# A hybrid decoder layer on one core: the first three column blocks in eight equal pieces, and the sample attention's cache tiles three to a visit

## The chip, the core and the metric

The kernel runs on one core of one Trainium2 chip. The time is device microseconds of one launch, median of 3 runs: 1757.73 us, between 1757.28 and 1758.61. One more execution, under the profiler, took 1758.0 us, and its span from the first to the last instruction is 1756.2 us.

In the profile PE is the tensor engine (matmuls), PEld its weight loads, DVE the vector engine, ACT the scalar engine, POOL the GpSimd engine, SP the engine that issues most loads and stores; a small q behind a name is that engine's own queue of DMA issues.

## The reference

One layer for a prompt group (256 tokens) and a sample group (8 sequences of 4 tokens), 288 tokens in all, in float32.

```python
z = jnp.einsum('ntd,de->nte', x, w_in)
h, gate_b, gate_c, q, k, v, g_a, g_b = jnp.split(z, _split_points(), axis=-1)

ya, conv_mix_new = _causal_dwconv(gate_c * h, conv_mix_prev, w_conv_mix)
ya = gate_b * ya
...
for g, (win, dil) in enumerate(GROUPS):
    ...
    o, l = _dilated_band_prompt(q[:, :, g], kg, vg, slopes[g], dil)   # prompt
    ...
    o, l = _dilated_band_sample(q[:, :, g], kg, vg, slopes[g], dil)   # sample: keys, values from a cache
wg = jax.nn.softmax(jnp.stack(lses), axis=0)
yb = jnp.einsum('gnth,gnthd->nthd', wg, jnp.stack(outs))

mixed = jax.nn.sigmoid(g_a) * (ya @ w_branch_a) + jax.nn.sigmoid(g_b) * (yb @ w_branch_b)
x1 = _layernorm(ALPHA * x + mixed @ w_out, ln1_g, ln1_b)
a, b = jnp.split(x1 @ w_up, 2, axis=-1)
a, conv_ffn_new = _causal_dwconv(a, conv_ffn_prev, w_conv_ffn)
y = _layernorm(ALPHA * x1 + (jax.nn.silu(a) * b) @ w_down, ln2_g, ln2_b)
```

The model width is 2048, the inner width of the last part 5632; there are 3 groups of 4 heads of 128. The old cache rows are also copied to the outputs.

## The kernel before, in words

**Layout.** Features lie on the 128 partitions, tokens along the free axis. Each token row is kept as two halves of 144 (dimensions h and a in the code: half and place in it). A matmul reads them interleaved ("p a h").

**Products.** Every weight matrix is cut into column blocks of 128. A block is 16 k-tiles of 128x128, 1 MB, loaded into a buffer `wst` (three of them, `prepare`, L169 on). Each float32 number is split in two parts: ACT rounds it to fp32r (`hi`), DVE subtracts that from the number (`lo`); `split`, L223, does it for weights and for activations. `product` (L197) then issues three matmuls for each k-tile: hi by hi, hi of the weights by lo of x, lo of the weights by hi of x (L217 to L219), 48 for a block, into one accumulator. Split weights go to half blocks `whi` and `wlo`, four buffers of each, so that the casts run up to two blocks ahead of PE. ACT's cast of a half block waits until PE has freed a buffer.

**The start.** PE first runs `N_WARM` matmuls on zeros (L235). The first three column blocks (0 and 1 together in `w_two`, 2 in `w_one`) are computed together as x arrives: `FIRST` cuts the 16 k-tiles into four pieces of two and two of four. For each piece there is a load of x (the first four on ACT's queue, the others on SP's), one of `w_two` and one of `w_one` (SP), then three casts on ACT in the order x, blocks 0 and 1, block 2, and three subtractions on DVE in that order. `first_three` (L285 is its matmul) goes piece by piece; in a piece it takes the three kinds of term one after the other, in each the k-tiles, and for each k-tile the three blocks. At its beginning it calls `prepare`, which issues the load of block 3 behind those loads on SP.

**What follows.** The q blocks (12, with the first three), then 24 blocks of k and v by head, each head followed by the prompt's attention in three parts spread over later products; then the gated convolution (48 blocks), the two branches with their gates, the output projection with a norm, and the up and down projections in three parts with the last norm.

**Sample attention.** It runs in between, as a generator (`sample_steps`) that `product` advances: 20 steps over the blocks from k on (`N_STEP`, `N_STEP_BLOCKS`), about one in five products. The old keys and values come as 18 tiles each of 128x2048 (`fetch_two`, L424: two at a time, each loaded into one of two `cache` buffers and then stored to the output from there, L425). For the scores, DVE masks q by batch (`by_batch`, one operation of 128x1024 for a group, L412), and PE multiplies with 32 columns of weights for each batch and head (L450), four heads beside each other in the array; the sums are picked and get their bias (`pick_t`, L431). After the last keys come the softmax, transposes (L483, L485, L493), and the same again with the values (L506), the last with the new values (L513). These matmuls are float32; each appears as two records in the trace. A group of matmuls that `in_a_row` ties together is called a visit here: PE leaves the stream of products for it. The first visit of a half reads two tiles with four batches each, the others two tiles with one batch each.

**SP's order.** All weight loads, cache loads and cache stores go through SP's queue in program order as scheduled; a store waits there for its load to land, a cache load for PE to be done with the buffer, a weight load for DVE to be done with it.

Of the kernel before, what the change touches and what calls it, by code (L numbers as in the profile page):

```python
# [11 lines left out]
F32R = mybir.dt.float32r  # L12
# [5 lines left out]
P = 128  # L18
# [11 lines left out]
HX = 160  # L30
# [23 lines left out]
C_M0 = C_TM + NT  # L54
C_M1 = C_M0 + NG * P
# [31 lines left out]
def layer_kernel(ctx: ExitStack, tc: tile.TileContext, ins, outs):  # L87
# [40 lines left out]
    spent = [0]  # L128
# [42 lines left out]
    def prepare():  # L171
# [24 lines left out]
    def product(x):  # L196

        w = w_ready.pop(0)
        if not w_ready:
            prepare()  # L200
        if steps_on[0]:
            spent[0] += N_STEP
            while spent[0] >= N_STEP_BLOCKS:
                spent[0] -= N_STEP_BLOCKS
                next(steps, None)
        o = acc(x[0].shape[-1])
        mms(o, w, x)
        prompt_step()
        return o.rearrange("p a h -> p h a")
# [27 lines left out]

    xh = sb(big, [P, KD, 2, HX], "xh", F32R)
    xl = sb(big, [P, KD, 2, HX], "xl", F32R)
# [6 lines left out]
    w_two_lo = [sb(wk, [P, 2, HK, P], "cache", F32R, bufs=2) for _ in range(2)]  # L246
# [4 lines left out]
    for k0, n, queue in FIRST:  # L251
        k = slice(k0, k0 + n)
        (act if queue == "act" else sp).dma_start(xs[:, k], x_in[:, k])
        sp.dma_start(w_two[:, :, k], w_in_two[:, :, k])
        sp.dma_start(w_one[:, k], w_in_one[:, k])
    splits = []
    for k0, n, _ in FIRST:
        k = slice(k0, k0 + n)
        splits.append(split(xh[:, k, :, :H], xl[:, k, :, :H], xs[:, k].rearrange("p k (a h) -> p k h a", h=2)))
        h = slice(k0 % HK, k0 % HK + n)  # L260
        splits.append(split(w_two_hi[:, :, k], w_two_lo[k0 // HK][:, :, h], w_two[:, :, k]))
        splits.append(split(w_one_hi[k0 // HK][:, h], w_one_lo[k0 // HK][:, h], w_one[:, k]))
    for before, after in zip(splits, splits[1:]):
        for i in range(2):
            behind(after[i], before[i])
# [3 lines left out]
    def first_three():  # L269
# [10 lines left out]
        for k0, n, _ in FIRST:  # L280
            for term in range(3):
                for k in range(k0, k0 + n):
                    xk = x[term == 1][:, k].rearrange("p h a -> p a h")
                    for b in range(3):
                        i = pe.matmul(  # L285
                            o[b], first_w(term == 2, b, k), xk, start=k == 0 and term == 0, stop=k == KD - 1 and term == 2
                        )
                        if before is not None:
                            behind(i, before)
                        before = i  # L290
        return [t.rearrange("p a h -> p h a") for t in o]

    cst = sb(big, [P, C_M0], "cst")
# [107 lines left out]
    bmask = cst[:, C_BM : C_BM + NB * NS].rearrange("p (b r) -> p b r", b=NB)  # L401
    tmask = cst[:, C_TM : C_TM + NT]

    sw = sb(wk, [P, NH * NB * NS + 1152], "sw", bufs=1)
    sw_m = sw[:, : NH * NB * NS].rearrange("p (j b r) -> p j b r", j=NH, b=NB)
    sw2 = sw[:, NH * NB * NS :]

    def by_batch(src):

        m = sw_m  # L410
        shape = [P, NH, NB, NS]
        dve.tensor_tensor(m, src.unsqueeze(2).broadcast_to(shape), bmask.unsqueeze(1).broadcast_to(shape), ALU.mult)  # L412
# [608 lines left out]
```

## Time and profile before

| | before |
|---|---|
| median of 3 runs | 1757.73 us (1757.28 to 1758.61) |
| profiled execution: time | 1758.0 us |
| profiled execution: span | 1756.2 us |
| PE busy | 1738.8 us, 99% |
| DVE busy | 1006.7 us, 57% |
| ACT busy | 797.9 us, 45% |
| POOL busy | 243.7 us, 14% |
| mean granted PE clock | 0.996 |
| read from and written to HBM | 389.89 MB and 94.53 MB |

How to read the lines below. A row of the timeline has the start, the duration, the engine and line, the operation, what it writes and reads, how many instructions were merged, and in brackets how long the engine stood idle before and what released it. A row of a group has the count, the shortest, median and longest duration in nanoseconds, and the first and the last start. Matmuls overlap in the array: a matmul of 288 columns has a duration of 286 ns while one starts every 0.12 us. A row of the chain of waits has a start, a time and what filled it; it shows the step from one matmul to the next. A row of waits has who waited for whom, the total in us, the number and the longest. A row of a stage (a window of the span) has the length, the busy time of PE, PEld, DVE, ACT and POOL with their instructions, the granted clock, the share of DMA time and GB/s.

### The profile page before, as it was taken

The page shows a single profiled execution, that of the slowest core. Times are in us where ns is not written, and L with a number is a line of the kernel's source. Part 1 is how long each engine was busy: PE and PEld are TensorE (multiplying, and loading weights), DVE is VectorE, ACT ScalarE, POOL GpSimd, SP SyncE. Part 2 cuts the span into 40 slices and gives each one's busy share as a digit, 9 for nine tenths or more (in the row PEclk, how much of TensorE's full clock was granted, in tenths as well). Part 3 has the DMA queues.
Part 4 walks back from the last instruction along what each step waited for, and adds up shares of the span by engine and source line. Part 5 has one row for each costly group of instructions (what it writes and reads, how often), then busy time and mean ns, then how long its engine had stood idle before and what let it go on. Part 6 is the DMA issues. An engine that isn't in the chain of part 4 may idle for free.

```text
span 1756.2 us, 33518 instructions
## 1 busy us (share of the span) xinstructions
PE 1738.8 (99%) x14257; PEld 1710.7 (97%) x14257; DVE 1006.7 (57%) x1278; ACT 797.9 (45%) x1142; POOL 243.7 (14%) x404
## 2 busy tenths in 40 slices
PE   9999999999999999999999999999999999999996
PEld 9999999999999999999999999999999999999996
DVE  5444445555555444455588888765555555555554
ACT  5444444334434333344455655544454443345444
POOL 0000000000000000001165333300011110011165
PEclk9999999999999999999999999999999999999998
DMA  9477787787787877477766656566666666666662
GB/s 330 170 287 274 274 307 283 280 326 282 299 322 272 319 300 264 150 252 264 259 251 224 231 219 231 224 226 230 224 232 221 235 218 238 219 236 217 225 217 102
DMA packets 61350, 436.25 MB, mean 248 GB/s; under 512 B 7312, under 2 KB 9360, under 8 KB 17296
## 3 DMA queue, kind: packets, MB, share of 16 engines
q1 hardware_dynamic: 59472, 429.40, 66.4%
q10 hardware_dynamic: 1728, 4.72, 0.7%
q8 instruction: 111, 1.82, 0.4%
q14 instruction: 39, 0.32, 0.1%
HBM read 389.89 MB, written 94.53 MB: 276 GB/s over the span
## 4 chain that ended last, share of the span: by engine, by line
PE 99%; DMA 0%; DVE 0%; ACT 0%; SPq 0%; ACTq 0%; issue 0%; DVEq 0%
PE acc L217 32%; PE acc L219 31%; PE acc L218 31%; PE long L506 1%; PE long L450 1%; PE acc L285 1%; DMA dd<-in_w_in 0%; PE att L391 0%; ACT yah L747 0%; DVE dd L723 0%; PE att L351 0%; PE acc L383 0%; PE att L349 0%; PE att L374 0%; PE att L687 0%; PE att L686 0%
## 5 line engine op out<-in xcount | busy, mean ns | idle before, releaser
L223 DVE TENSOR_TENSOR wlo<-wst,whi 128x1024 fp32r<-128x1024 f32 (+2 forms) x584 | 709.1, 1215 | 613.1 <-ACT whi L223 607.6
L223 ACT CAST whi<-wst 128x1024 fp32r<-128x1024 f32 (+2 forms) x584 | 593.3, 1017 | 888.0 <-PE acc L218 777.7
L217 PE MATMUL acc<-xh,whi 128*128 128x288 f32 (+1 forms) x3216 | 922.8, 287 | 0.0
L218 PE MATMUL acc<-xl,whi 128*128 128x288 f32 (+1 forms) x3216 | 920.4, 286 | 0.0
L219 PE MATMUL acc<-xh,wlo 128*128 128x288 f32 (+1 forms) x3216 | 920.3, 286 | 0.0
L217 PEld LDWEIGHTS acc<-xh,whi 128*128 128x128 f32 x3216 | 607.8, 189 | 10.3 <-ACT h L606 2.5
L218 PEld LDWEIGHTS acc<-xl,whi 128*128 128x128 f32 x3216 | 607.8, 189 | 0.2 <-issue 0.2
L219 PEld LDWEIGHTS acc<-xh,wlo 128*128 128x128 f32 x3216 | 607.8, 189 | 0.0
L217 PE MATMUL acc<-yah,whi 128*128 128x288 f32 x1216 | 347.9, 286 | 0.0
L219 PE MATMUL acc<-yah,wlo 128*128 128x288 f32 x1216 | 347.7, 286 | 0.0
L218 PE MATMUL acc<-yal,whi 128*128 128x288 f32 x1216 | 347.7, 286 | 0.0
L217 PEld LDWEIGHTS acc<-yah,whi 128*128 128x128 f32 x1216 | 229.7, 189 | 2.5 <-ACT h L628 2.5
L218 PEld LDWEIGHTS acc<-yal,whi 128*128 128x128 f32 x1216 | 229.8, 189 | 0.0
L219 PEld LDWEIGHTS acc<-yah,wlo 128*128 128x128 f32 x1216 | 229.8, 189 | 0.0
L584 POOL COPY qk_s<-u 128x2 f32<-128x2 f32 x44 | 38.1, 866 | 571.4 <-ACT u L798 448.6
L572 DVE SCALAR_TENSOR_TENSOR cy<-u,prm,cy 128x304 f32<-128x304 f32 x120 | 72.4, 603 | 3.8 <-ACT cy L570 0.7
L643 POOL TENSOR_TENSOR ya<-ya,dd 128x288 f32<-128x288 f32 x16 | 13.6, 850 | 306.0 <-DVE ya L642 306.0
L595 DVE TENSOR_TENSOR ya<-cy,acc 128x256 f32<-128x256 f32 x88 | 23.5, 310 | 33.8 <-PE acc L219 33.7
L223 ACT CAST yah<-ya 128x288 fp32r<-128x288 f32 x76 | 32.7, 430 | 16.6 <-DVE ya L600 8.5
L584 POOL COPY cm<-u 128x2 f32<-128x2 f32 x16 | 3.0, 185 | 256.5 <-DVE u L611 256.5
L677 POOL TENSOR_TENSOR cache<-cache,dd 128x288 f32<-128x288 f32 x29 | 29.1, 1002 | 52.6 <-DVE dd L763 33.6
L223 DVE TENSOR_TENSOR yal<-ya,yah 128x288 fp32r<-128x288 f32 x76 | 34.9, 460 | 1.3 <-ACT yah L223 1.1
(174 smaller groups left out, 830.2 us busy)
## 6 DMA issues: line engine op xcount, KB each, us to landing
wst<-in_w_in SPq DMA_DIRECT2D x113, 1024.0 KB, 6.2
wst<-in_w_up SPq DMA_DIRECT2D x88, 1024.0 KB, 4.8
wst<-in_w_down SPq DMA_DIRECT2D x32, 1024.0 KB, 4.8
cache<-in_ck SPq DMA_DIRECT2D x18, 1024.0 KB, 6.4
out_o_ck<-cache SPq DMA_DIRECT2D x18, 1024.0 KB, 10.1
cache<-in_cv SPq DMA_DIRECT2D x18, 1024.0 KB, 5.6
out_o_cv<-cache SPq DMA_DIRECT2D x18, 1024.0 KB, 9.4
wst<-in_w_a SPq DMA_DIRECT2D x16, 1024.0 KB, 6.1
```

The costliest lines, as they stand in the source:

```text
L217: pe.matmul(out, hi[:, c, :], xh_k, start=k == 0, stop=False)
L218: pe.matmul(out, hi[:, c, :], xl_k, start=False, stop=False)
L219: last_mm[0] = pe.matmul(out, lo[:, c, :], xh_k, start=False, stop=k == nk - 1)
L223: return act.copy(hi, src), dve.tensor_tensor(lo, src, f32(hi), ALU.subtract)
L285: i = pe.matmul(o[b], first_w(term == 2, b, k), xk, start=k == 0 and term == 0, stop=k == KD - 1 and term == 2)
L450: row.append(pe.matmul(p[j * NS : (j + 1) * NS], qm[:, j, b, :], c[:, o + j * cols : o + (j + 1) * cols], start=b == 0, stop=b == NB - 1,))
L506: row.append(pe.matmul(p[j * NS : (j + 1) * NS], sm[:, j, b, :], c[:, o + j * cols : o + (j + 1) * cols], start=b == 0 and g < 2, stop=b = ...
L572: dve.scalar_tensor_tensor(y, u[:, i : i + YW], prm[:, w0 + i : w0 + i + 1], y, ALU.mult, ALU.add)
L584: pool.tensor_copy(dst[:, 0:2], u[:, SEQ : SEQ + 2])
L595: dve.tensor_tensor(a, b, c, ALU.mult)
L643: pool.tensor_tensor(m, m, ma[:, i], ALU.add)
L677: pool.tensor_tensor(self.s1, self.s1, d, ALU.add)
```

## The change

The edits, by place:

- *Start.* Eight pieces of two k-tiles. The first two loads of x are on ACT's queue, with a small ACT copy (which brings the table load) between them; the other six are on SP, each ahead of its piece's weights. In the first piece, x is cast by k-tile on ACT and blocks 0 and 1 by k-tile on DVE; block 2 and all later pieces are cast on ACT. Subtractions are on DVE as before, and each of the two engines keeps one written-out order. In a piece and term, the matmuls of blocks 0 and 1 come first for both k-tiles, then those of block 2. One warm-up matmul fewer (17).
- *Block 3* is loaded in two halves.
- *x* lies tighter: its two halves start 145 elements apart instead of 160.
- *Sample attention.* Three tiles to a visit (`N_VISIT`), a visit every eight products (`APART`), from the seventh q product of the loop on; a cache load and its store go out in successive products; three `cache` buffers. Masks are one operation of 128x128 for each batch and tile, made two products ahead of the visit, from a mask table of 60 columns. The scratch `sw2` moves into the tail of `dd`. Some scores go to accumulators named `att` instead of `long`.
- The constants come in three loads instead of one.

The core of the diff:

```diff
-FIRST = ((0, 2, "act"), (2, 2, "act"), (4, 2, "act"), (6, 2, "act"), (8, 4, "sp"), (12, 4, "sp"))
-N_WARM = 18
-N_STEP = N_CT + 2
-N_STEP_BLOCKS = 2 * NG * NH + 5 * KD - 3
+N_PIECE = 2
+N_WARM = 17
+N_VISIT = 3
+APART = 8
...
-HX = 160
+HX = 2 * HG + 2
...
-        d = sp.dma_start(st[:, :nk, :], src.rearrange("p (k c) -> p k c", c=P))
+        for k0 in range(0, nk, HK if loads[0] == 1 else nk):
+            k = slice(k0, k0 + (HK if loads[0] == 1 else nk))
+            d = sp.dma_start(st[:, k, :], src[:, k])
...
         if steps_on[0]:
-            spent[0] += N_STEP
-            while spent[0] >= N_STEP_BLOCKS:
-                spent[0] -= N_STEP_BLOCKS
-                next(steps, None)
+            next(steps, None)
...
-    xh = sb(big, [P, KD, 2, HX], "xh", F32R)
+    xh = sb(big, [P, KD, HX], "xh", F32R)[:, :, : 2 * HG].rearrange("p k (h a) -> p k h a", h=2)
...
-    for k0, n, queue in FIRST:
-        k = slice(k0, k0 + n)
-        (act if queue == "act" else sp).dma_start(xs[:, k], x_in[:, k])
+    for k0 in range(0, KD, N_PIECE):
+        k = slice(k0, k0 + N_PIECE)
+        if k0 == N_PIECE:
+            i_table = act.copy(sb(wk, [P, 2], "wgb", bufs=2), f32(zero[:, :2]))
+        i_x = (act if k0 <= N_PIECE else sp).dma_start(xs[:, k], x_in[:, k])
+        if k0 == N_PIECE:
+            behind(i_x, i_table)
         sp.dma_start(w_two[:, :, k], w_in_two[:, :, k])
         sp.dma_start(w_one[:, k], w_in_one[:, k])
...
+        for n, (hi, lo, src) in enumerate(parts):
+            if k0 or n == 2:
+                casts.append(act.copy(hi, src))
+            else:
+                for c in range(N_PIECE):
+                    e = (slice(None),) * (1 + n) + (slice(c, c + 1),)
+                    if n == 0:
+                        casts.append(act.copy(hi[e], src[e]))
+                    else:
+                        rests.append(dve.tensor_copy(hi[e], src[e]))
+        rests += [dve.tensor_tensor(lo, src, f32(hi), ALU.subtract) for hi, lo, src in parts]
+    for row in (casts, rests):
+        for before, i in zip(row, row[1:]):
+            behind(i, before)
...
             for term in range(3):
-                for k in range(k0, k0 + n):
-                    xk = x[term == 1][:, k].rearrange("p h a -> p a h")
-                    for b in range(3):
+                for blocks in ((0, 1), (2,)):
+                    for k in range(k0, k0 + N_PIECE):
+                        xk = x[term == 1][:, k].rearrange("p h a -> p a h")
+                        for b in blocks:
...
-    def by_batch(src):
-        m = sw_m
-        shape = [P, NH, NB, NS]
-        dve.tensor_tensor(m, src.unsqueeze(2).broadcast_to(shape), bmask.unsqueeze(1).broadcast_to(shape), ALU.mult)
-        return m
+    def by_batch(n, src, b):
+        m = bmask[:, (NB - 1 - b) * NT : (NB - 1 - b) * NT + NS]
+        dve.tensor_tensor(sw_m[:, n], src, m.unsqueeze(1).broadcast_to([P, NH, NS]), ALU.mult)
...
-    def fetch_two():
-        for _ in range(2):
+    def fetch():
+        if to_store:
+            sp.dma_start(*to_store.pop())
+        elif len(cache_tiles) < N_VISIT:
             which, n = next(cache_left, (None, 0))
             if which:
-                t = sb(wk, [P, 2048], "cache", bufs=2)
+                t = sb(wk, [P, 2048], "cache", bufs=3)
                 behind(sp.dma_start(t, ins[which][n]), w_load[0])
-                sp.dma_start(outs["o_" + which][n], t)
+                to_store.append((outs["o_" + which][n], t))
                 cache_tiles.append(t)
...
+        held = [(0, range(4)), (0, range(4, NB))] + [(g, (b,)) for g in range(1, NG) for b in range(NB)]
...
+        for values in range(2):
+            p = [None] * NG
+            for first in range(0, N_CT, N_VISIT):
+                here = held[first : first + N_VISIT]
+                for n in range(APART):
+                    fetch()
+                    if values and first == 0 and n == 3:
+                        transposed()
+                    if n == APART - 2:
+                        at = 0
+                        for g, batches in here:
+                            for b in batches:
+                                by_batch(at, sT[:, g].rearrange("p (j r) -> p j r", j=NH) if values else q_s[:, g], b)
+                                at += 1
+                    yield
...
+                in_a_row(row)
...
+            steps_on[0] = j * NG + g >= NH * NG - 2 - APART // 2
...
-    steps_on[0] = True
```

More of the change, by code (lines that the diff above doesn't have):

```diff
@@ L54 @@
 C_M0 = C_TM + NT
+MASK = (2 * NB - 1) * NT
+C_MASK = C_BM + NS + NT - (NB - 1) * NT
 C_M1 = C_M0 + NG * P
@@ new lines, in sample_steps @@
+        for values in range(2):
[13 more added lines that the diff above has]
+                    yield
+                row = []
+                for g, batches in here:
+                    c = cache_tiles.pop(0)
+                    cols = P if g == 0 else NT * P
+                    for b in batches:
+                        if b == 0:
+                            p[g] = p[1] if values and g == 2 else att(P) if g == 0 else (
+                                att() if g == 2 else sb(ps, [P, cols], "long", bufs=1))
+                        o = (b % 4) * NH * P if g == 0 else 0
+                        for j in range(NH):
+                            row.append(pe.matmul(
+                                p[g][j * NS : (j + 1) * NS], sw_m[:, len(row) // NH, j], c[:, o + j * cols : o + (j + 1) * cols],
+                                start=b == 0 and not (values and g == 2), stop=b == NB - 1 and not (values and g < 2),
+                            ))
+                rest_of = [g for g, batches in here if NB - 1 in batches]
+                if values and 0 in rest_of:
+                    row += [
+                        pe.matmul(
+                            p[0][j * NS : (j + 1) * NS], sTn[:, j * NS : (j + 1) * NS], vn[:, j, :], start=False, stop=True
+                        )
+                        for j in range(NH)
+                    ]
+                elif not values and NG - 1 in rest_of:
```

187 lines of the change are left out of this document (77 added, 110 removed).

## The prediction

> **What bounds the kernel now.** I read the page first: span, busy times, the chain that ended last.
>
> ```profile
> span 1756.2 us, 33518 instructions
> ...
> PE 1738.8 (99%) x14257; PEld 1710.7 (97%) x14257; DVE 1006.7 (57%) x1278; ACT 797.9 (45%) x1142; POOL 243.7 (14%) x404
> ...
> PE 99%; DMA 0%; DVE 0%; ACT 0%; SPq 0%; ACTq 0%; issue 0%; DVEq 0%
> ```
>
> TensorE (PE) works for 1738.8 of 1756.2 us and carries 99% of the chain. So a change gains only where it removes PE time: holes in the PE stream, or matmul time itself. The view of waits, for PE alone, says how many holes have a releaser:
>
> ```profile
> PE acc L285 <- ACT yal L223: 0.7, 2, 0.4
> ```
>
> Of these waits all behind the first matmul belong to L285, the first three column blocks, and this is the largest. Everything after is an unbroken stream. What is left is that start, and what PE loses without waiting. For the start I took the timeline, and for its end the first and last start of the groups that write the accumulators:
>
> ```profile
> 0.73 1.89 ACTq L253 DMA_DIRECT2D yah<-in_x  x4
> 1.22 4.69 PE L235 MATMUL acc<-cy 128*128 128x288 f32 x18 [1.22 <-DVE cy L232]
> 2.65 1.28 ACT L223 ACT_TABLE_LOAD   x1 [2.65 <-issue]
> 5.05 0.72 ACT L223 CAST xh<-yah 128x576 fp32r<-128x576 f32 x1 [1.12 <-DMA yah<-in_x]
> 5.51 0.43 SPq L255 DMA_DIRECT2D wst<-in_w_in  x1
> 5.68 0.61 ACT L223 CAST yal<-dd 128x512 fp32r<-128x512 f32 x1
> 5.80 0.76 DVE L223 TENSOR_TENSOR xl<-yah,xh 128x576 fp32r<-128x576 f32 x1 [4.64 <-ACT xh L223]
> 6.35 0.51 PE L285 MATMUL acc<-xh,yal 128*128 128x288 f32 x2 [0.44 <-ACT yal L223]
> 6.48 0.68 DVE L223 TENSOR_TENSOR cache<-dd,yal 128x512 fp32r<-128x512 f32 x1
> 6.66 0.40 ACT L223 CAST whi<-wst 128x256 fp32r<-128x256 f32 x1 [0.37 <-DMA wst<-in_w_in]
> 7.10 0.43 DVE L223 TENSOR_TENSOR wlo<-wst,whi 128x256 fp32r<-128x256 f32 x1
> 7.12 0.39 PE L285 MATMUL acc<-xh,whi 128*128 128x288 f32 x1 [0.26 <-ACT whi L223]
> 7.35 0.41 PE L285 MATMUL acc<-xh,yal 128*128 128x288 f32 x2
> 8.97 0.62 ACT L223 CAST yal<-dd 128x512 fp32r<-128x512 f32 x1 [1.26 <-DMA dd<-in_w_in]
> 9.64 0.51 PE L285 MATMUL acc<-xh,yal 128*128 128x288 f32 x2 [0.29 <-ACT yal L223]
> ```
> ```profile
> L217 PE MATMUL acc<-xh,whi x3216: 286/286/391, 25.6 to 1667.8; 128*128 128x288 f32 x160, 128*128 128x290 f32 x30
> L235 PE MATMUL acc<-cy x18: 442/442/608, 1.2 to 5.5; 128*128 128x288 f32 x18
> ```
>
> Eighteen warm-up matmuls on zeros run from 1.22 on; the last starts at 5.5. The first piece of x arrives at 5.05. ACT casts x (0.72), then the weights of blocks 0 and 1 (0.61), and only then, at 6.35, can PE begin. At 7.12 it waits for the cast of block 2, at 9.64 for the second piece of weights, whose cast starts at 8.97 when its load lands. The next block's first matmul starts at 25.6.
>
> The chain of waits around one visit of the sample attention shows the other loss:
>
> ```profile
> 282.90 0.12 PE acc L218
> ...
> 283.76 0.12 PE acc L219
> 283.88 1.85 PE long L450 x16
> 285.73 0.32 PE acc L217
> 286.05 0.12 PE acc L218
> ```
> ```profile
> 284.26 0.13 PEld L450 LDWEIGHTS long<-cache,sw 128*32 128x32 f32 x4 [0.30 <-issue]
> 284.69 0.13 PEld L450 LDWEIGHTS long<-cache,sw 128*32 128x32 f32 x4 [0.30 <-issue]
> ```
>
> In the steady stream seven matmuls take 283.76 - 282.90 = 0.86 us, 0.123 each. The visit (16 narrow matmul records, two cache tiles) takes 1.85, and the matmul after it 0.32 instead of 0.12. Weight loads for its groups of four follow each other by 284.69 - 284.26 = 0.43, so its four groups are 1.72 of work. The visit thus costs 1.85 + 0.20 - 1.72 = 0.33 us that no work fills: about 0.13 going into the 32-column matmuls, 0.20 coming out.
>
> **The change, part by part.** The sum is made against the profiled execution: span 1756.2, time 1758.0; the median of the runs shown is 1757.73, 0.3 below it.
>
> *First three blocks.* They hold 8 pieces x 18 = 144 matmuls, 144 x 0.123 = 17.7 us without a hole. Now they take 25.6 - 6.35 = 19.25, so 1.55 us are holes and restarts.
>
> Start. Before, ACT puts four loads of x on its queue at once (0.73, 1.89 us long), and they share the engines with the weights. After, ACT issues the first piece of x (1.89/4 = 0.47), then runs the table load (1.28, now over near 2.5, hidden behind the wait for data as before), then issues the second; the others go on SP between the weights. The first x lands no later than 5.05. The first weights of blocks 0 and 1 have landed by 5.51 now (SP's next issue, which waits for them, goes at once); with three fewer x transfers beside them they land between 4.6 and 5.5; I take 5.4, because the second x, issued near 2.7, still runs beside them. VectorE then casts them by k-tile, while ACT casts x by k-tile: two casts in parallel where two stood in a row. A VectorE cast of 128x256 isn't in the trace. Nearest are its subtraction of that size (0.43) and ACT's cast of it (0.40) above, and its fill of 128x288 (0.30) below; I take 0.36. PE can start at 5.4 + 0.36 and some semaphore time, 5.8. The warm-ups, one fewer, end near 1.22 + 17 x 0.25 = 5.5 (0.25 = (5.5 - 1.22)/17), so they are no longer than the wait. Bounds of the start: 5.5 and 6.35 (nothing gained).
>
> Holes. In the first piece VectorE does its two casts (to about 6.1), then the subtraction for x (0.76), to 6.9. PE has six matmuls before it needs that: 5.8 + 6 x 0.123 = 6.5. Hole with restart 0.4; the subtractions after it (0.68, 0.43) keep ahead of six matmuls (0.74) each. Block 2's cast (0.40) on ACT follows the x casts and is wanted only as fifth, no longer third, since the changed order runs blocks 0 and 1 first. From the second piece on, casts cost ACT 0.72 + 0.61 + 0.40 = 1.73 and VectorE 0.76 + 0.68 + 0.43 = 1.87 a piece, against 18 x 0.123 = 2.21 on PE: both gain on it. Loads:
>
> ```profile
> 0.00:5.00 5.00, 3.78 (x16) 3.79 (x17) 0.30 (x1) 1.28 (x1) 0.62 (x8) 1.00 0.63 145
> 5.00:10.00 5.00, 4.00 (x25) 3.22 (x24) 2.86 (x5) 3.31 (x7) 0.00 (x0) 1.00 1.08 373
> 10.00:15.00 5.00, 5.00 (x43) 5.00 (x42) 4.64 (x9) 4.14 (x7) 0.00 (x0) 1.00 1.03 339
> 15.00:20.00 5.00, 5.00 (x42) 4.93 (x42) 3.77 (x4) 3.10 (x4) 0.00 (x0) 1.00 1.04 416
> 20.00:25.00 5.00, 4.99 (x41) 4.78 (x40) 2.84 (x3) 3.32 (x4) 0.72 (x1) 1.00 1.01 389
> ```
>
> The last column gives 0.73, 1.87, 1.70, 2.08, 1.95 MB per stage. A piece is 0.69 MB (x 288 KB, weights 384 KB), 1.8 us at the mean of 380 GB/s. Two pieces (1.38 MB) are in by 6.8, one each 1.8 us behind: always ahead of PE's 2.21. The hole at 9.64 came from four x loads in front of the second weights, and it goes. I take 0.3 us for all holes left, between 0 and 0.8 (half of those before). The first matmul of the next block then starts at 5.8 + 17.7 + 0.3 = 23.8, gain 1.8; at best 5.5 + 17.7 = 23.2, gain 2.4; at worst 6.35 + 17.7 + 0.8 = 24.8, gain 0.8.
>
> How the clock stands at the start belongs here. All 18 warm-ups have at least 442 ns, real ones 286 from 7.35 on, with 0.41 for two. So the rate doubled between 5.5 and 7.35. Real matmuls that start at 5.8 can be slow until 7.35 at most: 1.55/2 = 0.8 us lost, at least 0. I count 0.1 of it in the 0.3. The Trainium skill, TensorE: Matmul & The Clock Gate, section What's actually happening, says that the gate's window of 3413 ns is free-running and a busy one opens it; from 1.22 that is anything from 4.6 to 8.0, an estimate that speaks against an earlier start; by its middle (6.3) 0.25 us would be lost and the time 1754.2. The trace agrees as far as it goes.
>
> *What is late next.* Block 3 is wanted at 23.8. Its load now comes in two halves behind all pieces: 5.5 + 1.05 = 6.55 MB, which the stages above reach by about 20.5; casts on ACT take
>
> ```profile
> 22.91 2.00 ACT L223 CAST whi<-wst 128x1024 fp32r<-128x1024 f32 x2 [1.59 <-DMA wst<-in_w_in]
> ```
>
> 2.00 for two halves, so the first is there by 21.6 and its VectorE rest 1.2 later (the mask row below has that size), 1 us before PE wants it. SP issues 22 loads for these blocks where it issued 14; at 0.43 each (its row at 5.51) that is 9.5 us, less than the 14 us or so that their data take. The mask and constant loads behind them, three for one, are wanted tens of us later. If this cover went, each us that block 3 is late is one us of time.
>
> *Sample visits.* L450 is the key half, and the value half (L506) reads as many tiles:
>
> ```profile
> L450 PE MATMUL long<-cache,sw x192: 272/592/617, 142.6 to 410.9; 128*32 128x512 f32 x128, 128*32 128x128 f32 x64
> ```
>
> 128/16 = 8 visits of wide records and one of 64 narrow ones, 9 in each half, 18. With three tiles to a visit the same 36 tiles make 12. The work (6 groups of 0.43 a visit) stays; six times 0.33 = 2.0 goes, less 0.1 because two visits now stand right behind the prompt's float32 work and one will, so that fewer entries are saved: 1.9. Bounds: 6 x 0.20 = 1.2, and 2.0.
>
> Masks: 6 of 128x1024 become 48 of 128x128.
>
> ```profile
> L412 DVE TENSOR_TENSOR sw<-qk_s,cst x3: 1212/1214/1225, 81.1 to 286.7; 128x1024 f32<-128x1024 f32 x3
> ACT whi L223 <- PE acc L218: 777.7, 491, 4.1
> ```
>
> At least 1.214/8 = 0.15, at most 0.43 (the 128x256 above): 7 to 21 us for 7.3. It costs nothing because the weights' casts run ahead: ACT stood 777.7 us waiting for PE to free a buffer. Nine of them in a row, the most, are 4 us against about two half blocks (2 x 24 x 0.123 = 5.9) that lie ready. Each cache load now has a product between it and its store, so SP waits less with weights queued behind it; the third cache buffer lets loads start as a visit ends, as before. Starting the visits six products after the first three blocks puts their traffic where nothing waits for it.
>
> *No cost:* the scores' accumulators in other banks, the scratch moved into the tail of dd, the tighter x (half-step 145 elements instead of 160) change no count of matmuls; the last is priced below.
>
> Sum: 1.8 + 1.9 = 3.7. Span 1752.5, time 1754.3, and against the median 1757.73 - 3.7 = 1754.0.
>
> **Rivals.**
> 1. *The start goes at its best* (5.5, no hole, 2.4) and visits give 2.0: 1753.3. For it: all casts are shorter than PE's piece. Against it: VectorE's subtraction comes after two casts.
> 2. *The loads decide the start*: the second x on ACT's queue delays the first weights as much as three did, and the holes are halved at most: 0.8 + 1.9, 1755.0. For it: the first stage moved only 0.73 MB, little more than a piece.
> 3. *The visits don't do what they say*: the 0.33 belongs to a tile or its change of rows and not to a visit. Then 1.8 alone, 1755.9. Against it: the groups inside are an even 0.43 apart.
> 4. *Slower*: x's two halves lie 580 bytes apart instead of 640, so the halves of each pair that a matmul reads no longer lie alike. 9648 + 144 = 9792 matmuls read them (3 x 3216 and the first). From 3.7/9792 = 0.4 ns each the gain is gone, from 0.75 ns it is slower by over 0.2%. The nearest rows are a float32 group that reads every second element, with odd and even starts, and one that reads on end:
>
> ```profile
> L351 PE MATMUL att<-dd,yah x32: 273/276/277, 114.3 to 242.9; 128*128 128x128 f32 x32
> L391 PE MATMUL att<-yah,yal x64: 272/275/275, 134.8 to 266.0; 128*128 128x128 f32 x64
> ```
>
> 276 against 275 ns: taken as a price, 1 ns x 9792 = 9.8 us, 1763.8. Against it: the 32 have 273 to 277 with both starts, and the groups on yah (half-step 144) and xh (160) don't differ.
>
> **How the numbers follow.** Forecast 0.60, rivals 0.18, 0.09, 0.05, 0.08. About 0.2% (3.5 us, 1754.2) is what a measurement can tell here. The forecast's own range is 1753.0 to 1755.0, two thirds of it beyond 0.2%: 0.40, with rival 1 0.58 faster. The other 0.20 with rivals 2 and 3 is 0.34 within. Rival 4 is the 0.08 slower. The range 1752.4 to 1756.2 takes in the best start with some scatter of runs, and rivals 2 and 3; rival 4 stays out.
>
> **What would show it.** The first real matmul at 5.5 to 6.0 instead of 6.35; a wait of PE on VectorE's xl below 0.5 and none on the second weights; the first block of the steady loop at 23.2 to 24.2; no PE wait on a cast at block 3. Twelve rows of narrow matmuls, of about 2.75 us, each with one 0.32 behind it. A median of 286 ns and a step of 0.123 in the groups that read xh; 0.124 would be rival 4. The forecast is wrong if PE shows a wait anywhere after the first three blocks, or if the visits cost as much in sum as before.

## The result, and the profile after

| | before | after |
|---|---|---|
| median, runs beside each other on one chip | 1757.35 us (1756.95 to 1758.61, 19 runs) | 1754.21 us (1753.86 to 1754.69, 19 runs) |
| ratio after to before, 95% interval | | 0.9982 (0.9976 to 0.9988) |
| profiled execution: time, span | 1758.0 us, 1756.2 us | 1754.06 us, 1752.2 us |

The medians differ by 3.14 us, the two profiled executions by 3.94. The first lines of the page after, in the order of those of before:

```profile
span 1752.2 us, 33563 instructions
...
PE 1735.5 (99%) x14256; PEld 1710.4 (98%) x14256; DVE 1012.4 (58%) x1328; ACT 799.1 (46%) x1149; POOL 242.8 (14%) x404
...
PE 99%; DVE 0%; ACT 0%; DMA 0%; ACTq 0%; issue 0%; DVEq 0%
```

PE is still the bound, and carries 99% of the chain. The waits of PE in the profile after, all of them (who waited for whom, total, times, longest):

```profile
PE acc L238 <- DVE cy L235: 1.2, 1, 1.2
PE acc L308 <- DVE yal L283: 0.3, 1, 0.3
```

The first row is the wait ahead of the warm-ups, the second the one ahead of the first real matmul. The waits for the cast of block 2 and for the second piece of weights are gone, and no other has come. The start in the timeline of the kernel after:

```profile
1.22 4.17 PE L238 MATMUL acc<-cy 128*128 128x288 f32 x17 [1.22 <-DVE cy L235]
1.22 1.28 ACT L258 ACT_TABLE_LOAD   x1 [1.22 <-PEq L1045]
1.28 0.43 ACTq L259 DMA_DIRECT2D yah<-in_x  x1
...
5.01 0.81 ACT L281 CAST xh<-yah 128x288 fp32r<-128x288 f32 x2 [2.31 <-DMA yah<-in_x]
5.23 0.50 DVE L283 CAST yal<-dd 128x256 fp32r<-128x256 f32 x2 [4.07 <-DMA dd<-in_w_in]
...
5.67 0.73 PE L308 MATMUL acc<-xh,yal 128*128 128x288 f32 x4 [0.29 <-DVE yal L283]
5.72 0.41 ACT L275 CAST whi<-wst 128x256 fp32r<-128x256 f32 x1
...
6.24 0.46 PE L308 MATMUL acc<-xh,whi 128*128 128x288 f32 x2
...
6.67 0.54 PEld L308 LDWEIGHTS acc<-xl,yal 128*128 128x128 f32 x4 [0.19 <-DVE xl L284]
...
7.01 0.62 ACT L275 CAST yal<-dd 128x512 fp32r<-128x512 f32 x1
...
8.25 0.65 PE L308 MATMUL acc<-xh,yal 128*128 128x288 f32 x4
...
21.34 1.04 ACT L226 CAST whi<-wst 128x1024 fp32r<-128x1024 f32 x1 [0.71 <-DMA wst<-in_w_in]
22.61 1.05 ACT L226 CAST whi<-wst 128x1024 fp32r<-128x1024 f32 x1 [0.23 <-DMA wst<-in_w_in]
```

The first real matmul is at 5.67 (6.35 before), on x and weights that came at 5.0 and 5.23 and were cast side by side. The one hole left behind it stands at 6.67, where PE's weight load waits 0.19 for VectorE's subtraction for x. The second piece follows at 8.25 without a wait: its weights were cast at 7.01, where before they came at 8.97. Block 3 comes in two halves, cast from 21.34 and 22.61 on.

The groups that write the accumulators (count, shortest/median/longest in ns, first to last start):

```profile
L220 PE MATMUL acc<-xh,whi x3216: 285/286/391, 23.7 to 1663.9; 128*128 128x288 f32 x160, 128*128 128x290 f32 x30
L222 PE MATMUL acc<-xh,wlo x3216: 285/286/288, 23.9 to 1664.1; 128*128 128x288 f32 x160, 128*128 128x290 f32 x30
```

The steady loop begins at 23.7 instead of 25.6. One visit in the chain of waits after:

```profile
149.51 2.71 PE long L526 x24
152.22 0.32 PE acc L220
```

A visit is now 24 records in 2.71 us with one 0.32 behind it; there are 12. By the working used before it costs 2.71 + 0.20 - 6 x 0.43 = 0.33 us that no work fills, as much as a visit of two tiles did.

**Splitting the span.** Two cuts, at the end of the first three blocks and at the start of the last norm's last group of matmuls, separate the two halves of the change in any profile of this kernel. The first cut is the start and length of the last row of L285 (L308 after) in the chain of waits, the second a row near its end. In the kernel before, then after:

```profile
21.38 4.43 PE acc L285 x34
...
1740.03 0.98 PE att L687 x4
```
```profile
5.23 0.31 DVE yal L283
5.54 0.14 issue
5.67 18.18 PE acc L308 x144
...
1736.05 0.98 PE att L724 x4
```

Before: the start ends at 25.81, the stream between the cuts is 1740.03 - 25.81 = 1714.22 us, the rest 16.17. After: 23.85, 1712.20, 16.15. So of the 4.0 between the spans 1.96 came from the start, 2.02 from the stream and 0.02 from the rest. (The expectations below end the stream one group of matmuls, 1.0 us, earlier: 1713.2 and 1711.2.)

### The profile page after: what moved, and what is told of

Read it like the earlier page. It is cut to its first block, busy times and chain, and to the rows that moved or that the text cites. A ratio compares the mean times of both kernels' runs of the same rounds, so it can differ in the third digit from the quotient of the medians.

```text
span 1752.2 us, 33563 instructions
## 1 busy us (share of the span) xinstructions
PE 1735.5 (99%) x14256; PEld 1710.4 (98%) x14256; DVE 1012.4 (58%) x1328; ACT 799.1 (46%) x1149; POOL 242.8 (14%) x404
## 4 chain that ended last, share of the span: by engine, by line
PE 99%; DVE 0%; ACT 0%; DMA 0%; ACTq 0%; issue 0%; DVEq 0%
PE acc L220 32%; PE acc L221 31%; PE acc L222 31%; PE long L526 1%; PE acc L308 1%; PE att L526 1%; PE att L415 0%; DMA dd<-in_w_in 0%; ACT yah L784 0%; DVE dd L760 0%; PE att L375 0%; PE acc L407 0%; PE att L373 0%; PE att L398 0%; PE att L724 0%; PE att L723 0%
## 5 line engine op out<-in xcount | busy, mean ns | idle before, releaser
L226 DVE TENSOR_TENSOR wlo<-wst,whi 128x1024 fp32r<-128x1024 f32 (+1 forms) x578 | 705.0, 1220 | 595.3 <-ACT whi L226 592.3
L226 ACT CAST whi<-wst 128x1024 fp32r<-128x1024 f32 (+1 forms) x578 | 590.4, 1022 | 878.9 <-PE acc L221 772.0
L222 PE MATMUL acc<-xh,wlo 128*128 128x288 f32 (+1 forms) x3216 | 920.7, 286 | 0.0
L222 PEld LDWEIGHTS acc<-xh,wlo 128*128 128x128 f32 x3216 | 608.2, 189 | 0.0
L222 PE MATMUL acc<-yah,wlo 128*128 128x288 f32 x1216 | 347.9, 286 | 0.0
L222 PEld LDWEIGHTS acc<-yah,wlo 128*128 128x128 f32 x1216 | 229.9, 189 | 0.0
L680 POOL TENSOR_TENSOR ya<-ya,dd 128x288 f32<-128x288 f32 x16 | 13.7, 855 | 304.6 <-DVE ya L679 299.0
```

The source lines that it names most:

```text
L222: last_mm[0] = pe.matmul(out, lo[:, c, :], xh_k, start=False, stop=k == nk - 1)
L226: return act.copy(hi, src), dve.tensor_tensor(lo, src, f32(hi), ALU.subtract)
L680: pool.tensor_tensor(m, m, ma[:, i], ALU.add)
```

## The experiments

All were timed beside the kernel before on the same chip, in four sets. In these the kernel before has a median of 1757.16 (21 runs; experiments 1 to 3), 1757.74 (33 runs; 4 to 7), 1757.17 (33 runs; 8 to 11) and 1757.59 (15 runs; 12). Times are medians of 11 runs, and of one run in experiment 3.

**1. The start alone.** The kernel before with the changed start; visits, masks and the half-step of 160 as they were.

```diff
-FIRST = ((0, 2, "act"), (2, 2, "act"), (4, 2, "act"), (6, 2, "act"), (8, 4, "sp"), (12, 4, "sp"))
-N_WARM = 18
+N_PIECE = 2
+N_WARM = 17
...
```

> The kernel before with only the new start (eight pieces, order of loads, casts of the first piece on two engines, order of matmuls, 17 warm-ups, block 3 in two halves); the sample attention keeps its 18 visits. Theory A (two gains that add): the first matmul of the steady loop at 23.5 to 24.2, the stream behind it as long as before (1713.2 us to the end of the last product), time below the kernel before by 1.1 to 1.9, since 2.0 of the 3.1 us by which the medians differ are the visits'. Theory B (the profile's own start is typical): 1.9 below. Theory C (the start is worth nothing by itself): within 0.3 of the kernel before.

1756.09 (1755.65 to 1756.49), 1.07 below before; ratio 0.9993 (0.9984 to 1.0002). The interval reaches 1, but the slowest of these runs is below the fastest of the 21 beside them (1756.99). The gain is just under Theory A's 1.1 to 1.9. The chain of waits of this kernel:

```profile
5.59 18.19 PE acc L309 x144
...
1738.01 0.98 PE att L712 x4
```

Start ends at 23.78, stream 1714.23: the start of the kernel after, with the stream of the kernel before.

**2. The visits alone.** The kernel after with the start of the kernel before (the half-step stays at 145).

```diff
-N_PIECE = 2
-N_WARM = 17
+FIRST = ((0, 2, "act"), (2, 2, "act"), (4, 2, "act"), (6, 2, "act"), (8, 4, "sp"), (12, 4, "sp"))
+N_WARM = 18
...
```

> The changed kernel with the old start (pieces of 2, 2, 2, 2, 4, 4, four x loads on ACT's queue, all casts on ACT, 18 warm-ups, block 3 in one load); 12 visits and the rest of the change stay. Theory A: 12 visits with 0.33 us of entry and exit each, stream of 1711.2 us behind the start, time 2.0 below the kernel before (1755.3). Theory B: 1.2 below, if the profile's 1.9 for the start is typical and the medians' 3.1 is all there is. Rival 3 of the prediction (the overhead belongs to a tile): no change, 1757.3.

1755.59 (1755.22 to 1756.43), 1.57 below before; ratio 0.9990 (0.9982 to 0.9999). In the chain of waits of this kernel

```profile
9.56 16.00 PE acc L284 x126
...
1737.77 0.98 PE att L699 x4
```

the start ends at 25.56 and the stream is 1712.21. The gain by the medians lies between the two theories, while the stream is as short as Theory A has it. Added, the halves give 1.07 + 1.57 = 2.64 us. The whole change gave 3.14 in the runs of the result and 2.65 in the third set, so the medians show no more than that the sum is of this size. The profiles add up more closely: 25.81 - 23.78 = 2.03 from the start and 2.01 from the stream, against 4.0 between the spans.

**3. The kernel before once more**, for a second profile. No edit.

> The kernel before once more, to see how its start varies between executions. If Theory A holds, the profiled start of before (first steady matmul at 25.6) was 0.6 or so late, and this one comes at 24.8 to 25.6 with the same 1713.2 us behind it, so that the time follows the start; if Theory B holds it is 25.6 again and any difference of time lies elsewhere.

1757.71. Its start ended at 25.57, its stream was 1714.23: 0.24 earlier than in the first profile, for a time that is 0.29 lower. Like the first profile it lies above the median of its set, 1757.16.

**4. Two tiles to a visit.** Everything of the kernel after, but 18 visits again.

```diff
-N_VISIT = 3
-APART = 8
+N_VISIT = 2
+APART = 5
```

> The changed kernel with two tiles to a visit and a visit every five products (18 visits instead of 12); new start and all else as changed. If each visit costs 0.33 us of entry and exit: 1.6 to 2.0 above the changed kernel, the level of the new start alone (1756.1). If the overhead belongs to a tile: no difference. If part of the visits' gain came from masks, buffers or traffic: less than 1.2 above.

1756.28 (1755.88 to 1756.59), ratio 0.9992 (0.9983 to 1.0001), every run below every run of the kernel before in this set. In its chain of waits

```profile
5.66 18.40 PE acc L308 x144
...
1738.30 0.98 PE att L724 x4
```

the start ends at 24.06 and the stream is 1714.24, with six visits more 2.04 longer than after. What is paid belongs to the visit, not to the tile: rival 3 falls. Is it the float32 of the visit's matmuls or their 32 columns? A group of the prompt's attention in the kernel after is float32 too, with 128 columns of weights:

```profile
135.97 1.78 PE att L415 x16
137.75 0.12 PE acc L220
```

The matmul behind it takes its usual 0.12, where the one behind a visit takes 0.32. So the 0.20 on the way out comes with the narrow matmuls, not with float32.

**5. The halves of x 584 bytes apart** (146 elements; in the kernel after 145).

```diff
-HX = 2 * HG + 2
+HX = 146
...
-    xh = sb(big, [P, KD, HX], "xh", F32R)[:, :, : 2 * HG].rearrange("p k (h a) -> p k h a", h=2)
+    xh = sb(big, [P, KD, 2, HX], "xh", F32R)
```

> The changed kernel with x's two halves 146 elements apart (584 bytes) instead of 145 (580), so that both start at a multiple of 8 bytes; all else as changed. My theory: within 0.3 us of the changed kernel. Rival 4 of the prediction: matmuls that read the halves at 580 bytes pay tenths of a nanosecond each (9792 of them), and this one is 1 us or more faster.

1753.94 (1753.84 to 1754.74), ratio 0.998 (0.9971 to 0.9989): the runs overlap those of the kernel after in the other sets. In its chain of waits

```profile
5.67 18.41 PE acc L308 x144
...
1736.30 0.98 PE att L724 x4
```

the stream is 1712.22. The kernel after with the old 160, which had been planned, gave no time: there is no room for it beside three cache buffers. But kernels with 18 visits exist with both: 1714.22 and 1714.23 with 160 (before, start alone), 1714.24 with 145 (two tiles to a visit). Over the 9648 steady matmuls on xh or xl that is 0.002 ns each. Rival 4 falls.

**6. The first piece's casts all on ACT.**

```diff
-            if k0 or n == 2:
+            if True:
                 casts.append(act.copy(hi, src))
```

> The changed kernel with the first piece's casts all on ACT and uncut, as for the other pieces; all else as changed. If the two-engine cast is what the start gains from: ACT does x (0.73), then blocks 0 and 1 (0.6), PE starts 0.6 to 0.7 us later (6.3), and the time is 0.3 to 0.7 above the changed kernel (1754.5 to 1754.9); not all of the delay stays, since VectorE's subtraction, for which PE now waits at the seventh matmul, starts without its two casts ahead of it. If the order of loads alone makes the gain: within 0.2 of the changed kernel.

1754.61, ratio 0.9987 (0.9978 to 0.9996), but in two groups: seven of the eleven at 1754.17 to 1754.78, four at 1756.19 to 1756.39. The profiled execution was one of the lower group (1754.43); in its timeline

```profile
6.04 0.85 PE L308 MATMUL acc<-xh,yal 128*128 128x288 f32 x4 [0.37 <-ACT yal L275]
```

the first matmul waits 0.37 with PE idle, where the kernel after waited 0.29 and began 0.37 earlier. Its start ends at 24.25 (6.04 + 18.21), 0.40 later than in the first profile after. So the second engine's casts buy little in the lower group. An upper group was in neither expectation, and no execution of it was profiled; the next two kernels bear on what it is.

**7. Twelve warm-ups instead of 17.**

```diff
-N_WARM = 17
+N_WARM = 12
```

> The changed kernel with 12 warm-up matmuls instead of 17; they end at 1.22 + 12 x 0.25 = 4.2. The start gained 1.9 us between profiles but the medians differ by 1.1 for it. Theory W (in most executions the first piece lands earlier than in the profiled ones, and the 17 warm-ups hold the changed kernel back, but not the one before): 0.3 to 0.8 below the changed kernel. Theory D (PE waits for data in any case, near 5.6): the same time, or some tenths above it, if the idle gap keeps the clock low for longer.

1755.74, ratio 0.9988 (0.9980 to 0.9997): eight of eleven at 1755.41 to 1756.17, three at 1754.10 to 1754.48. The profile is of the upper group (1755.74). Its timeline, and stretches of half a us (length, PE's busy time with the matmuls that touch the stretch, granted clock, DMA share, GB/s):

```profile
5.86 1.30 PE L308 MATMUL acc<-xh,yal 128*128 128x288 f32 x4 [1.40 <-DVE yal L283]
```
```profile
6.50:7.00 0.50, 0.50 (x4) 1.00 1.04 376
...
9.00:9.50 0.50, 0.50 (x4) 1.00 1.05 379
9.50:10.00 0.50, 0.50 (x6) 1.00 1.12 368
```

PE sat idle for 1.40 us ahead of the first real matmul, and from 6.5 to 9.5 four matmuls touch each half us; then six. In the kernel after, six do from 6.0 to 6.5, four in the stretch with the hole at 6.67, and six or more from 7.0 on:

```profile
6.00:6.50 0.50, 0.50 (x6) 1.00 1.11 391
6.50:7.00 0.50, 0.50 (x4) 1.00 1.10 383
```

From 5.86 to 9.5 PE ran at half rate: by estimate 3.64/2 = 1.8 us lost. In the chain of waits the 144 matmuls took 19.69 us, 1.51 more than in the kernel after, and the stream is 1712.21 as there. So in this execution the doubling came late, behind an idle PE, and that is where its time went. The medians of the two groups (1755.79 and 1754.22) are 1.6 apart; that the other seven of the upper group lost it in the same way fits, but was not seen. Theory D had the cause, but forecast some tenths for it, not about 1.5 us.

**8. Casts on ACT, and 22 warm-ups**, so that the gap of experiment 6 is filled with warm-up matmuls.

```diff
-            if k0 or n == 2:
+            if True:
...
-N_WARM = 17
+N_WARM = 22
```

> The kernel with the first piece's casts on ACT alone and 22 warm-ups instead of 17. With 17, four of eleven executions stood 1.7 us above the others. Theory (PE's idle gaps at 5.7 to 6.0 and 6.6 to 6.8, while the rate is still half, put the doubling off by some 3.4 us, which costs half of that): 22 warm-ups last until 6.0 to 6.7 and cover the first gap, so no execution, or one at most, stands 1.5 us above the others, and the rest lie 0.2 to 0.8 above 1754.4. Rival (the upper group comes from the loads or from elsewhere): a third of the executions still stands at 1756.2 or above.

1754.45, all eleven at 1754.27 to 1754.96; ratio 0.9984 (0.9975 to 0.9992). There is no upper group; with 17 warm-ups four of eleven were in it. In the profiled execution the rate doubled during the warm-ups, so that the 22 ended at 6.04 and PE still idled for 0.21, but behind the doubling. The two kernels ran in different sets, each on its own chip. But the kernels of experiments 4 and 5, in the set of experiment 6, have no upper group either, and in their profiles PE does not idle ahead of its first real matmul. Beside the kernel after of the same set (below, 1754.52) there is no difference: with 22 warm-ups, casting on two engines is worth nothing that these runs can tell.

**9. The kernel after once more**, beside the others of the third set.

> The changed kernel once more, so that it stands on the same chip beside the others of this call: 1753.8 to 1754.7, 3.0 to 3.6 below the kernel before. In the profiled execution the first real matmuls may start at half rate (0.245 us each) until somewhere between 5.1 and 6.8, since the rate was seen to change at 5.1 to 5.4, near 6.0 and near 6.5 in other executions with the same 17 warm-ups.

1754.52 (1753.82 to 1754.66), ratio 0.9983 (0.9975 to 0.9992), 2.65 below the kernel before where 3.0 to 3.6 was expected. Its timeline and chain of waits:

```profile
5.66 1.14 PE L308 MATMUL acc<-xh,yal 128*128 128x288 f32 x4
6.43 0.40 ACT L275 CAST whi<-wst 128x256 fp32r<-128x256 f32 x1 [0.74 <-DMA wst<-in_w_in]
6.89 0.51 PE L308 MATMUL acc<-xh,whi 128*128 128x288 f32 x2
```
```profile
6.89 17.42 PE acc L308 x140
...
1736.51 0.98 PE att L724 x4
```

The first matmul is where it was in the first profile after (5.66), but the four take 1.14 instead of 0.73 us: half rate. And block 2's weights, whose cast started at 5.72 there, landed only at 6.43 here, so that the fifth matmul is at 6.89 instead of 6.24. The start ends at 24.31, 0.46 later; the stream is 1712.20 again.

**10. The first four loads of x on ACT's queue**, so ahead of the weights, as before.

```diff
-        i_x = (act if k0 <= N_PIECE else sp).dma_start(xs[:, k], x_in[:, k])
+        i_x = (act if k0 <= 3 * N_PIECE else sp).dma_start(xs[:, k], x_in[:, k])
```

> The changed kernel with the loads of x for the first four pieces on ACT's queue, as before (the other four stay on SP's); pieces, casts and order of matmuls as changed. If the order of need is what closed the hole at the second piece: a wait of PE on the cast of its weights returns (0.2 to 0.5 us near 8 to 9.5), time 0.3 to 1.0 above the changed kernel. If the casts and the order of matmuls are enough: within 0.2 of it.

1754.98 (1754.79 to 1755.67), ratio 0.9986 (0.9977 to 0.9995): every run is above every run of the kernel after in this set. The waits of PE and the timeline:

```profile
PE acc L308 <- ACT yal L275: 0.6, 1, 0.6
PE acc L308 <- ACT whi L275: 0.4, 1, 0.4
```
```profile
8.76 0.62 ACT L275 CAST yal<-dd 128x512 fp32r<-128x512 f32 x1 [1.28 <-DMA dd<-in_w_in]
9.43 0.76 PE L308 MATMUL acc<-xh,yal 128*128 128x288 f32 x4 [0.55 <-ACT yal L275]
```

The second weights land at 8.76, and the hole of before (at 9.64 there) is back at 9.43. The first matmul starts at 5.74 and the fifth at 6.90, behind the cast of block 2, much as in the profile of experiment 9 (5.66 and 6.89); so it is the second weights that make the difference. The order of need is worth 0.46 by the medians, and 0.82 between the profiled starts (25.13 against 24.31).

**11. A first piece of one k-tile**, so that PE has real work earlier (13 warm-ups).

```diff
-N_PIECE = 2
-N_WARM = 17
+PIECES = ((0, 1), (1, 1)) + tuple((k, 2) for k in range(2, 16, 2))
+N_WARM = 13
...
```

> The changed kernel with the first piece cut in two pieces of one k-tile (0.34 MB instead of 0.69) and 13 warm-ups, which end at 4.5. If data bound the start: the first real matmul near 4.9 instead of 5.6, and up to 0.6 us gained, less what is lost while the rate is still half (each matmul 0.12), so 0.1 to 0.4 below the changed kernel. If the rate is what counts: PE idles in the small pieces while the rate is still low, it stays low for longer, as with 12 warm-ups, and the time is 0.5 to 1.7 above in many executions.

1755.05 (1754.65 to 1755.44), ratio 0.9987 (0.9978 to 0.9995): 0.53 slower than the kernel after of the same set. In its timeline

```profile
4.50 0.68 PE L308 MATMUL acc<-xh,yal 128*128 128x288 f32 x2
...
8.82 0.76 PE L308 MATMUL acc<-xh,yal 128*128 128x288 f32 x4 [1.02 <-ACT yal L275]
```

real matmuls run from 4.50 on, but the first ones at half rate, and then PE waits 1.02 for the second pair of k-tiles: it has used up its work before the next loads come. The loads also came more slowly just then: from 4.5 to 6.5 they brought 211 GB/s, where the kernel after has 394. Why is not shown. So this run does not tell what an earlier start would gain if the data came as fast as before.

It does show something of experiment 7. Here only 13 warm-ups ran, one more than there, but real matmuls followed without a gap, and the doubling came near 6.2: the two matmuls from 6.06 take 0.35 us together, those from 6.41 on 0.12 each. No run is above 1755.44. So a small number of warm-ups does not by itself put the doubling off to 9.5; the idle stretch is what sets experiment 7 apart, with one profiled execution of each.

**12. The kernel before with 20 warm-ups**, to see whether a gap also explains the scatter of the kernel before.

```diff
-N_WARM = 18
+N_WARM = 20
```

> The kernel before with 20 instead of 18 warm-up matmuls, nothing else changed. Its profile shows a gap of 0.3 us between the warm-ups' end (5.91) and the first real matmul (6.24); two more at the unraised rate (about 0.25 us each) end at about 6.4 and close it. Theory (a gap of PE before the rate has doubled is what throws some executions of the kernel before back): its times lie in one group at 1756.9 to 1757.4, and none above 1757.6, where the kernel before beside it has several between 1757.5 and 1758.7. Rival (what scatters the kernel before has nothing to do with the warm-ups): the executions above 1757.5 are as frequent as beside it, all shifted by 0 to +0.2. Second rival (the first real matmuls are pushed back by the two extra): all lie 0.1 to 0.3 higher with the same scatter.

1757.56 (1756.98 to 1758.5) beside 1757.59; ratio 1.0 (0.9991 to 1.0009). Seven of eleven lie above 1757.5, beside it nine of fifteen. Its timeline shows why this decides less than it was meant to:

```profile
1.22 4.50 PE L235 MATMUL acc<-cy 128*128 128x288 f32 x20 [1.22 <-DVE cy L232]
6.34 0.51 PE L285 MATMUL acc<-xh,yal 128*128 128x288 f32 x2 [0.61 <-ACT yal L223]
```

In the profiled execution the rate doubled during the warm-ups, so that 20 of them ended earlier (5.72) than 18 had (5.91), and the gap was 0.61 and not closed. More warm-ups alone do not help this kernel; what scatters it stays open, and the first theory has no support here.

## Why the prediction was right, point by point

**The sum.** 1754.0 was forecast, 1754.21 measured, and in the profile a span of 1752.5 against 1752.2. That the times are only 0.2 apart is in part luck: the gain forecast, 3.7, was 0.56 more than the 3.14 between the medians, and the median it was taken from, 1757.73 of three runs, lay 0.38 above that of 19. The prediction gave 0.58 to a gain beyond 0.2% and 0.34 to one within it; the medians differ by 0.18%.

**Visits: right.** 1.9 forecast; the streams differ by 2.02, and 2.01 to 2.04 in each pair of kernels that differ in the visits. By 6, that is 0.34 for a visit, against the 0.33 read from one visit. The 0.1 taken off for entries behind the prompt's work was not seen. The Trainium skill, TensorEngine Tiling (Array Packing), section Key Properties, says that changing the tiling mode, not just the tile, drains TensorE, and gives no price. The trace agrees as far as it goes: a visit is one change to 32 columns and one back, and costs the same with two tiles between them and with three; the drain itself is not seen.

**First matmul: right, by other times.** 5.8 forecast, 5.67 (5.66 in the second profile after, 5.59 with the start alone, 5.46 and 5.48 in experiments 4 and 5). The weights landed at 5.23, not 5.4. VectorE's cast of 128x256 took 0.31 (5.23 to 5.54 in the chain), where 0.36 was taken between 0.43 and 0.30. The second x did not go out near 2.7, after the table load, but at 1.28, while that ran; so it ran beside the first weights for longer than assumed, and they came earlier all the same. The 17 warm-ups, forecast to end at 5.5 and so ahead of the data, ended at 5.39 in the first profile after, but at 5.67 in the second; in experiments 4 and 5, where the weights were there at 5.0, the real matmuls follow them without a wait.

**Holes: the term that was mis-sized.** 0.3 was forecast between 0 and 0.8, with 0.1 of it for the clock. The first profile after has 23.85 - 5.67 - 17.7 = 0.48, the second 24.31 - 5.66 - 17.7 = 0.95. The forecast hole at VectorE's xl was there (forecast 0.4, 0.19 idle at 6.67). What the second had more is the half rate of its first matmuls (1.14 - 0.73 = 0.41 more for the first four; in experiment 4 they took 1.29) and the late load of block 2. The clock is thus worth 0 to about 0.5 from one execution to the next, not 0.1. The Trainium skill, TensorE: Matmul & The Clock Gate, section What's actually happening, says that the gate's window is free-running. The trace agrees with a moment that changes from run to run: with 17 warm-ups the doubling came anywhere from near 5.3 (after) to near 6.6 (the second profile after), within the 4.6 to 8.0 that the prediction estimated from it. That the median, 1754.21, is also its 1754.2 for the middle of that window is no sign for it, since other terms of the sum missed by more.

**What the start gained.** 1.8 forecast, 1.96 between the two profiles, but only 3.14 - 2.02 = 1.12 by the medians, and 1.07 for the start alone. The profiled execution before, 1758.0, was 0.65 above the median of 19 runs, and that must lie in the start if, as in every profile, the stream repeats within 0.02 us. The forecast stood that profile 0.3 above the median of three runs, which was itself 0.38 above that of 19, and took the whole 1.8 from there. The forecast of the start after, 23.8, was right; what it was measured against was too late. No execution of the faster kind of the kernel before (1757.0 to 1757.3) was profiled, so where its start is shorter is not shown.

**Block 3: right, with less cover.** No wait. Its first half was to be cast by 21.6 and was by 22.38 (21.34 + 1.04), as the load landed later than the 20.5 estimated from the stages. VectorE's subtraction,

```profile
22.42 2.50 DVE L226 TENSOR_TENSOR wlo<-wst,whi 128x1024 fp32r<-128x1024 f32 x2 [1.00 <-ACT whi L226]
```

two of 1.25, has the first half done at 23.67, and the group of L222 starts at 23.9: 0.2 us ahead instead of 1.

**Masks: right.** A mask of 128x128 takes 0.286, between the bounds of 0.15 and 0.43:

```profile
L437 DVE TENSOR_TENSOR sw<-qk_s,cst x24: 283/286/350, 79.1 to 317.8; 128x128 f32<-128x128 f32 x24
```

The 24 of the value half have the same median. 48 of them are 13.7 us for the 7.3 of before, and PE shows no wait for any of it.

**Rivals.** 1 (the start at its best) asked for 23.2, which no profile shows. 2 (the loads decide) fell: with four loads of x on ACT's queue the time is 1754.98 against its 1755.0, but by another way, since the first matmul starts at 5.74 even there, so the first weights are not late, and the time is lost in the hole at the second weights. 3 and 4 fell by the lengths of the streams.

## What to carry to other kernels

- Where PE leaves a stream of wide matmuls for a few narrow ones, count the departures: each cost 0.33 us here with two tiles as with three, so the same 36 tiles in 12 visits instead of 18 gave 2.0 us.
- In a load-bound start, issue loads in the order in which the consumer needs them (0.46 us here), and keep PE busy without a gap until its real work comes: a gap ahead of the rate's doubling (1.40 us in one execution) can put the doubling off and cost more than its own length (about 1.8 us there).
- Cut a profile at fixed points and compare the pieces: a stream that repeats within 0.02 us settles a matter of 0.002 ns per matmul that runs that scatter by 0.8 us cannot, and shows in which piece an execution differs from its median.

## What the runs showed of the hardware

- A PE that idled ahead of the doubling of its rate lost more than the gap: with 1.40 us idle (12 warm-ups) the doubling came near 9.5 in the profiled execution, against 5.3 to 6.6 with 17, and near 6.2 with 13 and no gap (experiment 11). The times with 12 fall in two groups whose medians are 1.6 us apart. With the casts on ACT they are 2.0 apart (1754.27 and 1756.31); that this upper group has the same cause was not seen in a trace, but it was absent with 22 warm-ups.
- The column of the granted clock shows none of this: with 12 warm-ups it is 1.00 in the stretch from 6.50 to 7.00 with four matmuls as in that from 9.50 on with six. The rate is to be read from the step or the duration of the matmuls.
- A DMA that ACT issues went out while ACT's table load ran: at 1.28, within 1.22 to 2.50, though it stands in ACT's program behind the table load and behind the small copy that needs the table, which ran at 2.51. An order written behind that copy did not hold the load of x back here.
